# Two stacked sequence blocks on one core: other SBUF byte offsets for weights, rounded activations and hidden tiles, and the meta tokens' rounding moved to the first down product

## The chip, the cores and the metric

The kernel runs as one program on one core of one Trainium2 chip. The metric is the device time of that program in microseconds. Three runs of the kernel before took 1779.9, 1780.93 and 1783.77 us; their median is 1780.93 us.

## What is computed

Two blocks follow each other on 512 tokens of width 1024. The first mixes three branches (gated linear attention, a short convolution, windowed attention), then runs a gated feed-forward net with a causal convolution. The second puts 16 learned meta tokens ahead of the 512, runs two recurrent mixers (HGRN2 and Mamba-2) side by side, then a second feed-forward net. Cut to the matrix products that carry the time:

```python
u = rmsnorm(h, g_mix);  z = u @ w_in                    # 1024 -> 7440
merged = g1 * (o_gla @ w_gla_o) + g2 * (o_conv @ w_conv_o) + g3 * (o_swa @ w_swa_o)
h = h + merged @ w_o
h = h + (silu(conv(u @ w_up)[:, :2816]) * conv(u @ w_up)[:, 2816:]) @ w_down
h = concat([meta_tokens, h])                            # 16 + 512 tokens
proj = rmsnorm(h, norm1) @ w_in_2                       # 1024 -> 6672
h = h + concat([hgrn2(proj), mamba2(proj)]) @ w_out_2
h = h + conv_glu(rmsnorm(h, norm2) @ ffn_w_up) @ ffn_w_down
out = rmsnorm(h, final)[16:]
```

## The kernel before

Activations lie feature-major: 128 features on the partitions, tokens along the row, eight such tiles (index `k`) for the width of 1024. `H` is the residual in float32. Each product is taken in three passes on numbers cut to the engine's float32r format: an operand is split into a rounded high part and the rest (`XH` and `XL` for the normed input, `FH` and `FL` for the hidden layer of a feed-forward net, `MH` and `ML` for the merged branches, `bh_*` with `bl_*` or `blg*` for the three branch outputs, `yh` and `yl` for the mixers' outputs; `wh` and `wl` for the weights).

The weights come as a stream of 128x128 tiles, eight to a chunk of 512 KB. SyncE loads a chunk into `wraw` (line 69), ScalarE rounds it to `wh` (line 82), VectorE takes the rest to `wl` (line 83). A chunk is prepared two chunks before it is used.

`gemm` makes one output tile of 128 features. For each input tile `k` (a "k-step" below) `pass3` issues `(wh, xh)`, `(wh, xl)`, `(wl, xh)`: the weight tile is the stationary operand, and a row of 512 activations moves through it (line 179). So in block 1 a k-step is three matmuls of 512 columns. In block 2 the tokens are cut in two pieces, 256 and 258 columns or 264 and 264, so that a k-step there is six matmuls. Each matmul has a weight load of its own. In the profile a matmul `acc<-XH,wh` has `XH` as its moving operand and `wh` as its stationary one. Only the first product (`GV`) has it the other way round.

The order of the main stages on TensorE is: projections, branches and gates (to about 503 us), `w_up` (503 to 749), `w_down` (749 to 872), projections and mixers of block 2 with pieces of 264 and of 256 + 258 (872 to 1285), `w_out_2` (to 1379), `ffn_w_up_2` (to 1636), `ffn_w_down_2`.

Tiles get their place in SBUF from pools in the order in which the pools are opened and the tiles first asked for: `H`, `XH`, `XL`, the parameters, the constants `cm`, then `wraw`, `wh` and `wl`, then the small `stat` tiles, then whatever the stage needs. A constant or a pad more shifts all that follows it. `XH` and `XL` have a row of 528 tokens for each `k` (2112 bytes): 16 meta tokens in columns 0 to 15, the others from column 16 (`META`).

`split` is one ScalarE activation (high part) and one VectorE operation (rest). `meta_norm` is a generator: it is stepped in lane 1, between the k-steps of the first products, and it first splits the 16 meta columns of the eight `k` and then works out their norm. The calls are recorded, and a scheduler then sets each engine's order. In the first down product, `after(m, ...)` makes the new normed input of block 2 from each finished tile `m`.

Of the kernel before, what the change touches and what calls it, by code (L numbers as in the profile page):

```python
# [9 lines left out]
F32 = mybir.dt.float32  # L10
# [12 lines left out]
L = T + META  # L23
PADL = T + 32
KD = D // P
NFF = 22
# [100 lines left out]
class Builder:  # L127
    def __init__(self, ctx, tc, ins, out):
        self.tc, self.nc, self.ins, self.out = tc, tc.nc, ins, out
        nc = self.nc  # L130
        self.const = ctx.enter_context(tc.tile_pool(reuse_waits="tile", name="const", bufs=1))
        self.wraw = ctx.enter_context(tc.tile_pool(reuse_waits="tile", name="wraw", bufs=2))
        self.whl = ctx.enter_context(tc.tile_pool(reuse_waits="tile", name="whl", bufs=3))
        self.stat = ctx.enter_context(tc.tile_pool(reuse_waits="tile", name="stat", bufs=1))
        self.acc_p = ctx.enter_context(tc.tile_pool(reuse_waits="tile", name="accp", bufs=4, space=PSUM))
        self.sm_p = ctx.enter_context(tc.tile_pool(reuse_waits="tile", name="smp", bufs=4, space=PSUM))
        self.W = WStream(nc, ins["wts"], self.wraw, self.whl)
        self.lanes = [Lane() for _ in range(4)]
        self.hold = False
        self.pend = []  # L140
# [163 lines left out]
    def setup(self):  # L304
# [4 lines left out]
        self.par_t = c.tile([P, NPAR], F32, name="par_t")  # L309
        cm = c.tile([P, 3 * P + 16], F32, name="cm")  # L310
        self.four = cm[:, 3 * P:]
        self.ident, self.le, self.ones = (cm[:, i * P:(i + 1) * P] for i in range(3))
# [8 lines left out]
        nc.gpsimd.dma_start(out=self.par_t[:, 8:NPAR], in_=self.ins["par"][:, 8:NPAR])  # L321
        nc.gpsimd.dma_start(out=cm, in_=self.ins["cm"])
        nc.gpsimd.dma_start(out=self.H[:, :, 0:META], in_=self.ins["metaT"])
# [176 lines left out]
    def block1(self):  # L500
# [16 lines left out]
        for k in range(KD):  # L517
            self.split(XH[:, k, META:L], XL[:, k, META:L], H[:, k, META:L], self.par("g_mix", k))
            if k > 2:
                square(k - 3)  # L520
# [4 lines left out]
        Rx = R[:, META:L]  # L525
        segs = [(META, T)]
        X = self.X()
        WI = lambda c: [("w_in", k, c) for k in range(KD)]

        with ExitStack() as s1:  # L530
            br = self.br = s1.enter_context(tc.tile_pool(reuse_waits="tile", name="br", bufs=1))
            self.BH = {n: br.tile([P, 4, T], F32R, name=f"bh_{n}") for n in ("gla", "conv", "swa")}
            self.BL = {n: br.tile([P, 4, T], F32R, name=f"bl_{n}") for n in ("conv", "swa")}
            blg = self.blg = [None] * 4
# [5 lines left out]
            with ExitStack() as s2:  # L540
# [14 lines left out]
                with tc.tile_pool(reuse_waits="tile", name="sp", bufs=1) as sp:  # L555
# [6 lines left out]
                    for k in range(KD):  # L562
                        wh, wl = self.W.take([("w_in", k, GV + m * P) for m in range(4)])
                        for b in range(4):
                            c = slice(META + b * P, META + (b + 1) * P)
                            for i, (x, w) in enumerate(((XH, wh), (XL, wh), (XH, wl))):
                                self.mm(accs[b], x[:, k, c], w, start=k == 0 and i == 0, stop=k == 7 and i == 2)
# [4 lines left out]
                    def ev_gv(a):  # L572
                        for b in range(4):
# [3 lines left out]
                    self.lanes[1].add(self.meta_norm(), 6)  # L577
                    self.gemm16(wga, self.par("g_mix", 0, KD), segs, 3,
                                lambda a: self.mul(self.GAt[0:96], a[0][0:96], Rx[0:96]))
# [56 lines left out]
            mp = s1.enter_context(tc.tile_pool(reuse_waits="tile", name="mp", bufs=1))  # L636
            MH = mp.tile([P, KD, T], F32R, name="MH")
            ML = mp.tile([P, KD, T], F32R, name="ML")
            for m in range(KD):
# [20 lines left out]
            for m in range(KD):  # L660
                def ev_o(a, m=m):
                    h = H[:, m, META:L]
                    self.add(h, h, a[0])
                    self.split(XH[:, m, META:L], XL[:, m, META:L], h, self.par("g_ffn", m))
                    self.sumsq(sqa, m, h)
# [7 lines left out]
        def after(m, h, _):  # L673
            self.split(XH[:, m, META:L], XL[:, m, META:L], h, g1[:, m:m + 1])
            self.sumsq(sqh, m, h)
            self.ts(h, h, self.par("g_final", m), ALU.mult)
            self.sumsq(sqg, m, h)
# [3 lines left out]
    def ffn(self, up, cw, cb, down, R, after, zero):  # L681
        nc, tc, H = self.nc, self.tc, self.H
        W = T + 2
        segs = [(META, T)] if zero else [(META - 2, 256), (META + 254, 258)]
        Xb = (self.XH, self.XL)
        with tc.tile_pool(reuse_waits="tile", name="fp", bufs=1) as fp:
            FH = fp.tile([P, NFF, T], F32R, name="FH")
            FL = fp.tile([P, NFF, T], F32R, name="FL")
            for j in range(NFF):
                cs = []  # L690
                for i in range(2):
# [6 lines left out]
                    def ev(a, i=i, f=f, u=u, c=c, cs=cs, j=j):  # L698
                        o = 2 if zero else 0
                        for ps, (c0, n) in zip(a, segs):  # L700
                            self.mul(u[:, o:o + n], ps[:, 0:n], R[:, c0:c0 + n])
# [38 lines left out]
    def meta_norm(self):  # L740
        nc, H, st = self.nc, self.H, self.stat
        for k in range(KD):
            self.split(self.XH[:, k, 0:META], self.XL[:, k, 0:META], H[:, k, 0:META], self.par("norm1", k))
            yield 1
        sq = st.tile([P, L], F32, tag="sqt", name="msq", bufs=1)[:, 0:KD * META].rearrange("p (k t) -> p k t", t=META)
# [757 lines left out]
```

## Time and profile before

| | |
|---|---|
| median of three runs | 1780.93 us |
| the profiled execution's own time | 1779.66 us |
| its span | 1777.8 us |
| TensorE (PE) busy | 1747.9 us, 98% |
| weight loads (PEld) busy | 1535.7 us, 86% |
| VectorE (DVE) busy | 1092.6 us, 61% |
| ScalarE (ACT) busy | 728.9 us, 41% |
| moved from HBM | 156.93 MB, 89 GB/s |

The busy time of TensorE counts the union of its matmuls, whose ends are modelled and overlap. What a matmul costs in a dense stream is read from the distance between the starts of two matmuls in the timeline; below that is called the pitch, and the distance between the starts of two k-steps the length of a k-step. The rows round starts to 10 ns, the trace keeps them to 1 ns.

### The profile page before, as it was taken

How to read it: one execution, taken by the hardware profiler on the slowest of the kernel's cores; microseconds unless marked ns; L12 is line 12 of the kernel's file. 1: busy time of each engine (PE TensorE's matmuls, PEld its weight loads, DVE VectorE, ACT ScalarE, POOL GpSimd, SP SyncE). 2: the span in 40 equal slices, each digit the busy share in tenths (PEclk: the TensorE clock that was granted, in tenths of full speed). 3: DMA queues.
4: the chain of work that ended last, by engine and by line, in shares of the span. 5: the costliest groups of instructions: out<-in, count | busy, mean ns of one | idle time of the engine just before them, and what ended most of it. 6: DMA issues, size and time to landing. Idle time of an engine off the chain costs nothing. (4 is left out here: it accounts for less than half of the span.)

```text
span 1777.8 us, 26968 instructions
## 1 busy us (share of the span) xinstructions
PE 1747.9 (98%) x11014; PEld 1535.7 (86%) x11014; DVE 1092.6 (61%) x1923; ACT 728.9 (41%) x1175; POOL 124.8 (7%) x203
## 2 busy tenths in 40 slices
PE   8999999999999999999998999999999999999997
PEld 6777778888888888888898999999999999999775
DVE  5476774444457777733488789767633676676332
ACT  5356342222344444423356545555432444344221
POOL 2000000000110000001112221000001000000000
PEclk9999999999999999999999999999999999999998
DMA  5221223332333333233233322222222223323321
GB/s 184 84 72 60 72 74 93 95 95 93 95 95 95 95 95 95 95 95 95 86 100 128 115 83 72 69 71 69 73 91 88 91 87 93 96 88 91 95 88 66
DMA packets 45691, 160.84 MB, mean 90 GB/s; under 512 B 5472, under 2 KB 5616, under 8 KB 45568
## 3 DMA queue, kind: packets, MB, share of 16 engines
q1 hardware_dynamic: 42480, 149.83, 27.6%
q0 software_dynamic: 2800, 9.03, 1.6%
q8 instruction: 86, 1.41, 0.3%
q14 instruction: 37, 0.30, 0.1%
q10 hardware_dynamic: 288, 0.27, 0.0%
HBM read 156.93 MB, written 2.18 MB: 89 GB/s over the span
## 5 line engine op out<-in xcount | busy, mean ns | idle before, releaser
L179 PE MATMUL acc<-XH,wh 128*128 128x512 f32 (+3 forms) x2320 | 632.2, 326 | 0.1
L179 PE MATMUL acc<-XL,wh 128*128 128x512 f32 (+3 forms) x2320 | 621.6, 321 | 0.0
L179 PE MATMUL acc<-XH,wl 128*128 128x512 f32 (+3 forms) x2320 | 621.5, 322 | 0.0
L82 ACT CAST wh<-wraw 128x1024 fp32r<-128x1024 f32 (+1 forms) x279 | 291.6, 1045 | 520.0 <-PE acc L179 453.5
L83 DVE TENSOR_TENSOR wl<-wraw,wh 128x1024 fp32r<-128x1024 f32 (+1 forms) x279 | 341.7, 1225 | 220.4 <-ACT wh L82 213.3
L179 PEld LDWEIGHTS acc<-XH,wh 128*128 128x128 f32 x2320 | 385.7, 189 | 44.9 <-issue 9.7
L179 PEld LDWEIGHTS acc<-XH,wl 128*128 128x128 f32 x2320 | 386.2, 189 | 33.8 <-issue 0.5
L179 PEld LDWEIGHTS acc<-XL,wh 128*128 128x128 f32 x2320 | 385.5, 188 | 33.0 <-issue 0.5
L179 PE MATMUL acc<-FH,wh 128*128 128x512 f32 x352 | 140.3, 399 | 0.0
L179 PE MATMUL acc<-FH,wl 128*128 128x512 f32 x352 | 138.9, 395 | 0.0
L179 PE MATMUL acc<-FL,wh 128*128 128x512 f32 x352 | 138.6, 394 | 0.0
L162 DVE SCALAR_TENSOR_TENSOR c<-u,par_t,c 128x512 f32<-128x512 f32 x176 | 131.9, 749 | 6.8 <-ACT c L176 3.7
L150 DVE TENSOR_TENSOR u<-acc,R 128x512 f32<-128x512 f32 (+2 forms) x132 | 63.8, 510 | 91.2 <-PE acc L179 88.1
L334 POOL TENSOR_TENSOR sqa<-sqa,sqt 128x512 f32<-128x512 f32 x27 | 40.9, 1515 | 745.9 <-ACT sqt L176 745.9
L179 PEld LDWEIGHTS acc<-FH,wl 128*128 128x128 f32 x352 | 66.1, 188 | 16.5
L179 PEld LDWEIGHTS acc<-FL,wh 128*128 128x128 f32 x352 | 66.1, 188 | 15.6
L179 PEld LDWEIGHTS acc<-FH,wh 128*128 128x128 f32 x352 | 66.1, 188 | 15.3
L176 ACT ACTIVATE FH<-c 128x512 fp32r<-128x512 f32 x44 | 27.8, 632 | 116.5 <-DVE c L150 116.5
L150 DVE TENSOR_TENSOR H<-H,acc 128x512 f32<-128x512 f32 (+2 forms) x41 | 22.6, 569 | 77.7 <-PE acc L179 77.7
L176 ACT ACTIVATE c<-u,par_t 128x512 f32<-128x512 f32 x88 | 67.7, 769 | 2.6 <-DVE u L150 2.5
L176 ACT ACTIVATE c<-c 128x512 f32<-128x512 f32 x44 | 27.8, 632 | 85.1 <-DVE c L162 85.0
L179 PE MATMUL acc<-yh,wh 128*128 128x256 f32 (+1 forms) x256 | 51.4, 283 | 0.1
(393 smaller groups left out, 1969.6 us busy)
## 6 DMA issues: line engine op xcount, KB each, us to landing
wraw<-in_wts SPq DMA_DIRECT2D x277, 512.0 KB, 3.6
seg<-cumd POOLq DMA_DIRECT2D x10, 512.0 KB, 4.5
H<-in_xT SPq DMA_DIRECT2D x8, 256.0 KB, 9.1
ei<-eid POOLq DMA_DIRECT2D x16, 128.0 KB, 3.2
out<-H SPq DMA_DIRECT2D x7, 256.0 KB, 2.7
wraw<-in_wts SPq DMA_DIRECT2D x2, 256.0 KB, 4.4
r<-in_r POOLq DMA_DIRECT2D x1, 272.0 KB, 3.7
r<-in_r POOLq DMA_DIRECT2D x1, 256.0 KB, 7.5
```

What stands on the lines that cost most here:

```text
L82: self.nc.scalar.copy(h[:, e], t[:, e])
L83: self.nc.vector.tensor_tensor(out=l[:, e], in0=t[:, e], in1=h[:, e].bitcast(F32), op=ALU.subtract)
L150: self.nc.vector.tensor_tensor(out=out, in0=a, in1=b, op=op)
L162: self.nc.vector.scalar_tensor_tensor(out=out, in0=a, scalar=s, in1=b, op0=op0, op1=op1)
L176: self.nc.scalar.activation(out=out, in_=a, func=func, scale=scale, **kw)
L179: self.nc.tensor.matmul(out, lhsT, rhs, start=start, stop=stop)
L334: self.nc.gpsimd.tensor_tensor(out=acc, in0=acc, in1=t, op=ALU.add)
```

## The change

Five pieces of layout change, and one piece of work moves.

- `cm` has 8 columns more (32 bytes), which are never used. All that lies behind it moves up by 32 bytes: `wraw`, `wh`, `wl`.
- `stat` gets a pad of 160 bytes; what lies behind it moves by 192 bytes in all.
- A pad of 512 bytes stands between the high and the low tiles of the branches, of `M` and of `F`.
- In block 1 the rounded input lies in columns 8 to 519 of `XH` and `XL` (`X1 = 8`) and no longer in 16 to 527. Block 2 uses the columns it used before.
- Since columns 8 to 15 then hold tokens of block 1, the split of the 16 meta tokens can't stand in `meta_norm` any longer. It is made tile by tile in `after` of the first down product.

```diff
+X1 = 8
...
+        self.stat.tile([P, 40], F32, name="pad0")
...
-        cm = c.tile([P, 3 * P + 16], F32, name="cm")
-        self.four = cm[:, 3 * P:]
+        cm = c.tile([P, 3 * P + 24], F32, name="cm")
+        self.four = cm[:, 3 * P:3 * P + 16]
...
-        nc.gpsimd.dma_start(out=cm, in_=self.ins["cm"])
+        nc.gpsimd.dma_start(out=cm[:, 0:3 * P + 16], in_=self.ins["cm"])
...
-            self.split(XH[:, k, META:L], XL[:, k, META:L], H[:, k, META:L], self.par("g_mix", k))
+            self.split(XH[:, k, X1:X1 + T], XL[:, k, X1:X1 + T], H[:, k, META:L], self.par("g_mix", k))
...
-        segs = [(META, T)]
+        segs = [(X1, T)]
...
             self.BH = {n: br.tile([P, 4, T], F32R, name=f"bh_{n}") for n in ("gla", "conv", "swa")}
+            br.tile([P, P], F32, name="pad1")
...
             MH = mp.tile([P, KD, T], F32R, name="MH")
+            mp.tile([P, P], F32, name="pad2")
             ML = mp.tile([P, KD, T], F32R, name="ML")
...
         def after(m, h, _):
             self.split(XH[:, m, META:L], XL[:, m, META:L], h, g1[:, m:m + 1])
+            self.split(XH[:, m, 0:META], XL[:, m, 0:META], H[:, m, 0:META], self.par("norm1", m))
...
-        segs = [(META, T)] if zero else [(META - 2, 256), (META + 254, 258)]
+        segs = [(X1, T)] if zero else [(META - 2, 256), (META + 254, 258)]
+        rsegs = [(META, T)] if zero else segs
...
             FH = fp.tile([P, NFF, T], F32R, name="FH")
+            fp.tile([P, P], F32, name="pad3")
             FL = fp.tile([P, NFF, T], F32R, name="FL")
...
     def meta_norm(self):
         nc, H, st = self.nc, self.H, self.stat
-        for k in range(KD):
-            self.split(self.XH[:, k, 0:META], self.XL[:, k, 0:META], H[:, k, 0:META], self.par("norm1", k))
-            yield 1
```

The two built programs give each tile its byte address in a partition. From these, for each product, the offset of the moving row from the weight tile, taken modulo 256 bytes (all `wh` and `wl` buffers lie a multiple of 4096 bytes apart, and weight tiles 512 bytes, so there is one offset for each row):

| moving rows | start modulo 256, before | offset from the weights, before | start, after | offset, after |
|---|---|---|---|---|
| `wh`, `wl` themselves | 192 | | 224 | |
| `XH`, `XL` in block 1, `k` = 0, 1, 2, 3 (then again) | 192, 0, 64, 128 | 0, 64, 128, 192 | 160, 224, 32, 96 | 192, 0, 64, 128 |
| `bh`, `bl`, `blg`, `MH`, `ML`, `FH`, `FL` | 32 | 96 | 224 | 0 |
| `XH`, `XL` in block 2, pieces of 264 | 128 + 64k; 160 + 64k | 192 + 64k; 224 + 64k | the same | 160 + 64k; 192 + 64k |
| `XH`, `XL` in block 2, pieces of 256 and 258 | 184 + 64k | 248, 56, 120, 184 | the same | 216, 24, 88, 152 |
| `yh8` to `yh15` | 32 and up by 32 | 96, 128, 160, 192, 224, 0, 32, 64 | 224 and up by 32 | 0, 32, ... 224 |
| `yh0` to `yh7` | 160 and up by 64 | 224, 32, 96, 160 (twice) | 96 and up by 64 | 128, 192, 0, 64 (twice) |

From `XH` to `XL` it is 16,896 bytes before and after (512 modulo 1024); between the high and low tiles of `M` and `F` it was a multiple of 1024, and is now 512 bytes more.

The order of TensorE's matmuls is the same, but for the two matmuls of the meta tokens' norm, which stand some 25 rows earlier. On the two engines that make the splits, the order changes at the start and at the end of `w_up`.

VectorE at the start of the program, from the third chunk of weights on, before (`XL<-H,par_t,XH 128x16` is a meta split, `sqa<-sqa,R` adds a square to the sum for the norm, `wl<-wraw,wh` is the low part of a chunk):

```order
L83 TENSOR_TENSOR wl<-wraw,wh 128x1024
L162 SCALAR_TENSOR_TENSOR XL<-H,par_t,XH 128x512 x4
L516 TENSOR_TENSOR sqa<-sqa,R 128x512
L162 SCALAR_TENSOR_TENSOR XL<-H,par_t,XH 128x512
L516 TENSOR_TENSOR sqa<-sqa,R 128x512
L83 TENSOR_TENSOR wl<-wraw,wh 128x1024
L516 TENSOR_TENSOR sqa<-sqa,R 128x512
L162 SCALAR_TENSOR_TENSOR XL<-H,par_t,XH 128x16
L83 TENSOR_TENSOR wl<-wraw,wh 128x1024
L162 SCALAR_TENSOR_TENSOR XL<-H,par_t,XH 128x16 x6
```

and the same place after:

```order
L84 TENSOR_TENSOR wl<-wraw,wh 128x1024
L164 SCALAR_TENSOR_TENSOR XL<-H,par_t,XH 128x512 x4
L518 TENSOR_TENSOR sqa<-sqa,R 128x512
L164 SCALAR_TENSOR_TENSOR XL<-H,par_t,XH 128x512
L518 TENSOR_TENSOR sqa<-sqa,R 128x512 x2
L84 TENSOR_TENSOR wl<-wraw,wh 128x1024 x2
```

The seven meta splits here are gone, and the third sum now stands ahead of the chunk's low part instead of behind it.

ScalarE at the same place, before (`R<-H` and `sqt<-H` are squares, `wh<-wraw` rounds a chunk):

```order
L176 ACTIVATE XH<-H,par_t 128x512 x2
L176 ACTIVATE R<-H 128x512
L176 ACTIVATE XH<-H,par_t 128x512 x3
L176 ACTIVATE R<-H 128x512
L176 ACTIVATE XH<-H,par_t 128x16 x2
L82 CAST wh<-wraw 128x1024
L176 ACTIVATE sqt<-H 128x512
L176 ACTIVATE R<-H 128x512
```

and after:

```order
L178 ACTIVATE XH<-H,par_t 128x512
L178 ACTIVATE R<-H 128x512
L178 ACTIVATE XH<-H,par_t 128x512 x3
L178 ACTIVATE R<-H 128x512
L178 ACTIVATE XH<-H,par_t 128x512
L178 ACTIVATE R<-H 128x512
L83 CAST wh<-wraw 128x1024
L178 ACTIVATE sqt<-H 128x512
```

The rounding of the chunk now stands behind the third square instead of two meta splits.

VectorE at the end of `w_up`, after (`c` is a convolution's sum; before, the `128x16` rows are not there and the rest stands in the same order):

```order
L164 SCALAR_TENSOR_TENSOR c_5417<-u,par_t,c_5417 128x512
L164 SCALAR_TENSOR_TENSOR XL<-H,par_t,XH 128x16
L164 SCALAR_TENSOR_TENSOR c_5417<-u,par_t,c_5417 128x512
L164 SCALAR_TENSOR_TENSOR XL<-H,par_t,XH 128x16 x6
L152 TENSOR_TENSOR u<-acc,R 128x512
L84 TENSOR_TENSOR wl<-wraw,wh 128x1024
L164 SCALAR_TENSOR_TENSOR c_5456<-u,par_t,c_5456 128x512
L164 SCALAR_TENSOR_TENSOR XL<-H,par_t,XH 128x16
```

The scheduler has pulled the eight meta splits from `after` ahead, to the last two column groups of `w_up`.

## Rows read from the trace of the kernel before

**Rows 1.** The page, busy time, share of the span and instructions of each engine.

```profile
PE 1747.9 (98%) x11014; PEld 1535.7 (86%) x11014; DVE 1092.6 (61%) x1923; ACT 728.9 (41%) x1175; POOL 124.8 (7%) x203
```

**Rows 2.** Window of `w_down`: busy us of PE, PEld, DVE, ACT, POOL, granted clock, DMA.

```profile
749.10:872.20 123.10, 123.10 (x529) 99.05 (x528) 49.14 (x48) 36.97 (x45) 17.07 (x12) 1.00 0.31 94
```

**Rows 3.** Groups by line and shape: count, busy us, mean ns, idle before.

```profile
L179 PE MATMUL acc<-XH,wh 128*128 128x512 f32 x784 | 312.5, 399 | 0.0
L179 PE MATMUL acc<-FH,wh 128*128 128x512 f32 x352 | 140.3, 399 | 0.0
L179 PE MATMUL acc<-MH,wh 128*128 128x512 f32 x64 | 25.5, 399 | 0.0
L179 PE MATMUL acc<-bh_gla,wh 128*128 128x512 f32 x32 | 12.7, 398 | 0.0
L179 PE MATMUL acc<-XH,wh 128*128 128x256 f32 x544 | 156.4, 288 | 0.0
```

**Rows 4.** Timeline of TensorE, gates of block 1: start us, length, engine, line.

```profile
443.80 0.39 PE L179 MATMUL acc<-XH,wh 128*128 128x512 f32 x1
...
444.49 0.40 PE L179 MATMUL acc<-XH,wh 128*128 128x512 f32 x1
...
445.19 0.40 PE L179 MATMUL acc<-XH,wh 128*128 128x512 f32 x1
...
445.89 0.39 PE L179 MATMUL acc<-XH,wh 128*128 128x512 f32 x1
...
446.58 0.39 PE L179 MATMUL acc<-XH,wh 128*128 128x512 f32 x1
```

**Rows 5.** Timeline of TensorE, `w_down`: starts of its first two column groups.

```profile
749.09 0.39 PE L179 MATMUL acc<-FH,wh 128*128 128x512 f32 x1
...
764.48 0.40 PE L179 MATMUL acc<-FH,wh 128*128 128x512 f32 x1
```

**Rows 6.** Timeline of TensorE, `w_out_2`: starts of `yh8` to `yh15`, `yh0`, next group.

```profile
1356.26 0.40 PE L179 MATMUL acc<-yh,wh 128*128 128x256 f32 x2
...
1356.97 0.40 PE L179 MATMUL acc<-yh,wh 128*128 128x256 f32 x2
...
1357.70 0.40 PE L179 MATMUL acc<-yh,wh 128*128 128x256 f32 x2
...
1358.40 0.40 PE L179 MATMUL acc<-yh,wh 128*128 128x256 f32 x2
...
1359.13 0.40 PE L179 MATMUL acc<-yh,wh 128*128 128x256 f32 x2
...
1361.98 0.40 PE L179 MATMUL acc<-yh,wh 128*128 128x256 f32 x2
...
1367.70 0.40 PE L179 MATMUL acc<-yh,wh 128*128 128x256 f32 x2
```

**Rows 7.** Timeline of TensorE, `ffn_w_up_2`: two starts that lie 32 k-steps apart.

```profile
1503.17 0.40 PE L179 MATMUL acc<-XH,wh 128*128 128x256 f32 x2
...
1526.32 0.40 PE L179 MATMUL acc<-XH,wh 128*128 128x256 f32 x2
```

**Rows 8.** Timeline at the start, TensorE: a matmul that waited for weights.

```profile
20.45 0.50 PE L179 MATMUL acc<-wl,XH 128*128 128x512 f32 x1 [0.64 <-DVE wl L83]
```

**Rows 9.** Timeline at the start, VectorE: a sum of squares, the weights' low part.

```profile
17.31 0.69 DVE L516 TENSOR_TENSOR sqa<-sqa,R 128x512 f32<-128x512 f32 x1
...
19.18 1.22 DVE L83 TENSOR_TENSOR wl<-wraw,wh 128x1024 fp32r<-128x1024 f32 x1
```

**Rows 10.** Timeline at the start, ScalarE: two meta splits, the weights' high part.

```profile
17.60 0.49 ACT L176 ACTIVATE XH<-H,par_t 128x16 fp32r<-128x16 f32 x2
18.00 1.03 ACT L82 CAST wh<-wraw 128x1024 fp32r<-128x1024 f32 x1
```

**Rows 11.** Timeline of VectorE: six meta splits early; the last hidden tile.

```profile
23.24 1.99 DVE L162 SCALAR_TENSOR_TENSOR XL<-H,par_t,XH 128x16 fp32r<-128x16 f32 x6
...
754.28 0.69 DVE L150 TENSOR_TENSOR FL<-c,FH 128x512 fp32r<-128x512 f32 x1 [0.70 <-ACT FH L176]
```

More of the change, by code (lines that the diff above doesn't have):

```diff
@@ L564, in block1 @@
                         for b in range(4):
-                            c = slice(META + b * P, META + (b + 1) * P)
+                            c = slice(X1 + b * P, X1 + (b + 1) * P)
                             for i, (x, w) in enumerate(((XH, wh), (XL, wh), (XH, wl))):
@@ L577, in block1 @@
                     self.lanes[1].add(self.meta_norm(), 6)
-                    self.gemm16(wga, self.par("g_mix", 0, KD), segs, 3,
+                    self.gemm16(wga, self.par("g_mix", 0, KD), [(META, T)], 3,
                                 lambda a: self.mul(self.GAt[0:96], a[0][0:96], Rx[0:96]))
@@ L663, in ev_o @@
                     self.add(h, h, a[0])
-                    self.split(XH[:, m, META:L], XL[:, m, META:L], h, self.par("g_ffn", m))
+                    self.split(XH[:, m, X1:X1 + T], XL[:, m, X1:X1 + T], h, self.par("g_ffn", m))
                     self.sumsq(sqa, m, h)
@@ L699, in ev @@
                         o = 2 if zero else 0
-                        for ps, (c0, n) in zip(a, segs):
+                        for ps, (c0, n) in zip(a, rsegs):
                             self.mul(u[:, o:o + n], ps[:, 0:n], R[:, c0:c0 + n])
```

## The prediction

> **What bounds the kernel now.** I read the busy shares first. TensorE has a matmul in flight for 98% of the span, VectorE and ScalarE for 61% and 41% [rows 1]; a stage view of `w_down` shows the same picture with the full granted clock of 1.00, which is the upper of TensorE's two levels, 2.4 GHz [rows 2]. So the time is the sum of TensorE's pitches, and other engines count only where TensorE waits for them. Next I read the timeline for the pitch itself. At 2.4 GHz 512 columns would take 213.3 ns. A column group of `w_down` has 22 k-steps of three matmuls and takes 764.48 - 749.09 = 15.39 us, 233 ns a matmul [rows 5]. No engine is named as releaser in there, and the length repeats: of 336 undisturbed k-steps of `w_down`, 332 take 700 ns to the nanosecond. So some 20 ns of each matmul is surplus that no wait explains.
>
> Then I asked what changes the surplus. In block 1 the k-steps on `XH` and `XL` have the same three matmuls of 512 columns, but a cycle of lengths: 690, 698, 697 and 695 ns for `k` = 0, 1, 2, 3, the same for 4 to 7, and so on through all of `w_up` (0.69, 0.70, 0.70, 0.69 in the rounded rows [rows 4]; the first value stands in 163 of 179 undisturbed steps). What goes round with period four in `k` is the address of the moving row: a row of 2112 bytes moves it by 64 modulo 256. The weights meanwhile move by 512 a step, and `FH` by 2048 while its pitch never changes. So a period of 256 bytes fits, and I take the offset of the moving row from the weight tile loaded beside it as the variable. The tables of the change then say what is wanted: offset 0 gives 690 ns, 64, 128 and 192 give 698, 697 and 695, and 96 gives 700, the worst seen in these steps.
>
> **The change part by part.**
>
> *Branches, `M` and `F`: offset from 96 to 0.* There are 352 k-steps on `F`, 64 on `M` and 3 x 32 on the branches [rows 3], 512 in all. The nearest row for offset 0 is the first step of the `XH` cycle, 690 ns [rows 4], against 700 now [rows 5]. 512 x 10 ns = **-5.1 us**. Bounds: if the 690 belongs to its place in the cycle and not to its offset, these steps get the cycle's mean, 695, which is -2.6; if the fourth step's luck is better, 687 ns (three pitches of 229, the best steady stretch I find, in the first product at 17 to 19 us), -6.7. The pads of 512 bytes cost nothing themselves. They leave offsets modulo 256 as they are, so in this sum they are worth nothing either.
>
> *`XH` and `XL` in block 1.* The rows go down by 32 bytes and the weights up by 32: the offsets are 192, 0, 64, 128, the same four values in the same order, one step later. The cycle of 2.78 us for four steps [rows 4] should stay: **0**, with 784 k-steps [rows 3] at stake, 1.6 us either way for 2 ns a step. The pieces of 264 in block 2 swap the offsets of their two halves: 0.
>
> *`XH` and `XL` in pieces of 256 and 258.* These are 544 k-steps [rows 3], most of them in `ffn_w_up_2`, where 32 take 23.15 us, 723 ns each [rows 7]. Their offsets now lie 8 bytes below multiples of 64, and will lie 8 bytes below odd multiples of 32. The trace has no step like that, and the neighbours are the steps of `w_out_2`, which have the same shapes on `yh` and `yl`. There the high tile's offset climbs by 32: 96, 128, 160, 192 take 0.71, 0.73, 0.70 and 0.73 us [rows 6]. Over all sixteen tiles the odd multiples of 32 average 714 ns and the multiples of 64 721. The steps in question, at 723, are like the latter; moved to the former they would gain 7.6 ns. 544 x 7.6 = **-4.1 us**. The ends are 0 (the 8 bytes matter more than the rest, since no `yh` starts there) and 20 ns a step, the distance to the best `yh` step, -10.9. I take the middle value, as the mean of twelve rows.
>
> *`w_out_2`.* `yh8` to `yh15` keep their set of offsets. `yh0` to `yh7` now stand on odd multiples of 32 and take (1367.70 - 1361.98) / 8 = 715 ns [rows 6]; they come to multiples of 64, 721. 64 steps x 6 ns = **+0.4 us**.
>
> *The start.* TensorE waits 0.64 us for a chunk's low part [rows 8]. That operation runs 19.18 to 20.40 on VectorE [rows 9], behind the chunk's rounding on ScalarE, 18.00 to 19.03 [rows 10]. Now the third square stands ahead of the rounding in place of two meta splits. It reuses the buffer that the sum of 17.31 reads until 18.00 [rows 9], so it runs 18.0 to 18.6, the rounding 18.6 to 19.6, and the low part, behind the third sum, 19.8 to 21.0. **+0.6 us**; 0 if the square finds its buffer earlier. Later chunks have some microseconds to spare, and the norm's matmuls are only moved to where their inputs are long done.
>
> *The moved meta splits.* Eight on ScalarE, eight on VectorE. Six took 1.99 us on VectorE [rows 11], so eight are 2.7 us there, less on ScalarE, and no DMA or other queue. They now stand in the last two column groups of `w_up`. Behind them on ScalarE waits the rounding of a chunk that is needed two chunks later; behind them on VectorE waits the last hidden tile, finished at 754.97 [rows 11] and needed in the last k-step of the group that ends at 764.48 [rows 5]. With 2.7 us more it still has 6: 0. Without that cover it would be 2.7.
>
> The sum: -5.1 - 4.1 + 0.4 + 0.6 = **-8.2 us**. Against the profiled execution's own 1779.66 that is 1771.5. The median of the runs is 1.3 higher, so on that footing I expect **1772.7 us**.
>
> **The rivals.** A measurement of this kernel tells about 0.2%, or 3.6 us, from no change.
>
> *Only the hidden tiles gain.* The 8 bytes decide the pieces of 256 and 258, and nothing is won there: -4.1, 1776.8. For it: their four steps do not rank as the `yh` steps do (the one at offset 184 is the slowest, 735 ns).
>
> *Addresses don't matter.* The differences are those of the tensors, or of the place in the stream, and only the start shows: +0.6, 1781.5. Against it speaks the cycle of four in `XH` [rows 4], which has one tensor, one shape and nothing else that goes round by four. The Trainium skill, "TensorE: Matmul & The Clock Gate", section "Step-by-step: what each phase is for", says so by its rule: moving operand and weight load have a read port each, and loading the next weights takes nothing from the running matmul. By that rule the time would be that of this rival; the trace does not agree, as far as the cycle is a matter of addresses.
>
> *Slower: the start within 64 bytes.* Suppose the mechanism is not the distance but where a row starts: rows at 0 modulo 64 (`XH` in block 1, 695 on average) against rows at 32 modulo 64 (`F`, `M`, branches, 700). The change puts all of block 1's `XH` rows at 32 modulo 64 and leaves the others there: 784 x 5 ns = +3.9, with the start +4.5, 1785.4. It decides if the fetch of a row pays for the piece it shares with its neighbour. Against it: the `yh` steps that start at 32 modulo 64 are the faster ones [rows 6], and the halves of 264, one at 0 and one at 32, have the same mean pitch within 0.5 ns.
>
> **How the numbers follow.** The forecast gets 0.46, the hidden tiles alone 0.21, no effect 0.17, slower 0.09; 0.07 are left for a larger gain than any row shows, by the pads or by the steady stretches settling better, around 1764. Faster by over 0.2% is below 1777.4: 0.95 of the forecast, 0.6 of the second case, and the large gain, 0.63 in all. Slower by over 0.2% is the one rival, 0.09. The rest, 0.28, is within. The range goes from 1764.5, with the good ends of both main terms (-6.7 and -10.9) less what else is uncertain, to 1782.5, which takes in the case without effect. The forecast's own range is 1766 to 1777.
>
> **What would show it.** The k-steps of `w_down` should take 690 ns, a column group 15.2 us instead of 15.39, and those of the gates and `w_up` still cycle with 2.78 us for four. 32 k-steps of `ffn_w_up_2` should take 22.9 us instead of 23.15. At the start TensorE should wait about 1.2 us for `wl` near 20 us. If `w_down` stays at 700 the offset is the wrong variable. If four steps on `XH` take 2.80 or more, the start within 64 bytes was the cause. A wait of TensorE near 764 us would show that the meta splits were not covered.

## The result and the profile after

The changed kernel takes **1769.26 us** (median of four runs, 1768.26 to 1771.67) against 1780.95 before (1779.90 to 1783.77); the ratio is 0.9936, with a 95% interval from 0.9924 to 0.9949. That is 11.4 us less, where 8.2 were forecast; the time lies in the forecast's own range.

The profiled execution took 1771.67 us, the slowest of its four, with a span of 1769.8 us against 1777.8. So the two traces differ by 8.0 us only, and the reason stands in the table: TensorE runs the same 9360 products of rounded operands in the same order in both kernels, so the start of each can be set against its counterpart. The differences, by stage:

| stage | before, us | after, us | difference | forecast |
|---|---|---|---|---|
| to the end of the first product | 36.80 | 38.56 | +1.8 | +0.6 |
| projections, branches, `M` (64 + 96 k-steps at 700) | 465.76 | 463.12 | -2.6 | -1.6 |
| `w_up` (352 k-steps on `XH`) | 246.53 | 246.53 | 0.0 | 0 |
| `w_down` (176 k-steps on `FH`) | 123.20 | 119.73 | -3.5 | -1.8 |
| block 2 up to `w_out_2` | 412.39 | 413.79 | +1.4 | -1.5 |
| `w_out_2` | 94.48 | 94.35 | -0.1 | +0.4 |
| `ffn_w_up_2` (352 k-steps of 256/258) | 257.11 | 254.83 | -2.3 | -2.7 |
| `ffn_w_down_2` to the end (176 k-steps on `FH`) | 141.55 | 138.94 | -2.6 | -1.8 |

(The forecast's two main terms are shared out here by k-steps.) The line that does not fit is the stage of block 2 with its many small operations, +1.4. There TensorE waits for VectorE at the same three places in both traces. First before, then after; the columns are start, length, engine, line, operation, and in brackets the wait with its releaser:

```profile
955.53 0.77 PE L182 MATMUL sm<-cm,xf 128*128 128x128 f32 x5 [1.92 <-DVE xf L162]
966.26 0.77 PE L182 MATMUL sm<-cm,xf 128*128 128x128 f32 x5 [1.51 <-DVE xf L162]
977.34 0.77 PE L182 MATMUL sm<-cm,xf 128*128 128x128 f32 x5 [1.88 <-DVE xf L162]
```

```profile
951.87 0.77 PE L184 MATMUL sm<-cm,xf 128*128 128x128 f32 x5 [2.75 <-DVE xf L164]
962.66 0.77 PE L184 MATMUL sm<-cm,xf 128*128 128x128 f32 x5 [1.58 <-DVE xf L164]
973.92 1.09 PE L184 MATMUL sm<-cm,xf 128*128 128x128 f32 x5 [2.08 <-DVE xf L164]
```

The waits are 1.1 us longer. The rest comes from the granted clock. 0.3 us after the end of the third wait it fell to 0.50, the lower of TensorE's two levels (1.2 GHz), for 3.4 us, while before kept 1.00 here; so the five matmuls of the last row take 1.09 us instead of 0.77. The same stretch of matmuls, from the end of this wait on, takes 2.66 us before (first row) and 4.24 after (second row); the third row is the time at the lower level:

```profile
977.34:980.00 2.66, 2.66 (x28) 2.33 (x29) 2.62 (x4) 2.63 (x8) 0.00 (x0) 1.00 0.29 34
973.92:978.16 4.24, 4.24 (x29) 3.71 (x29) 2.75 (x4) 2.99 (x8) 0.00 (x0) 0.60 0.42 124
974.23:977.64 3.41, 3.41 (x26) 3.05 (x24) 2.22 (x3) 2.68 (x7) 0.00 (x0) 0.50 0.45 125
```

In all, the stretch from 872 to 1000 us of before's time is 2.4 us longer. The profiles of the kernels below sort by this fall of the clock and not by their addresses: the two without one (`e2_pad0`, `e5_x16`) have the stretch 0.7 to 0.8 us shorter than before, the three with one or two falls in it have it longer, by 1.2 (`e7_row576_8`), 1.3 (`e4_weights`) and, with two falls and nothing but before's addresses, 3.1 us (`e3_move`). In `e6_row576` the fall comes behind the stretch, which is 0.6 us shorter. The mean granted clock of the changed kernel's other three executions, 1768.26 to 1769.91 us, is 0.998, where this one has 0.997. So I do not count this stretch to the change. Without it the stages give -10.4 for this pair of executions, and the medians -11.7.

Now the profile itself. Busy shares, to be set beside [rows 1]: 9.9 us less of TensorE, the rest as before.

```profile
PE 1738.0 (98%) x11014; PEld 1534.6 (87%) x11014; DVE 1089.8 (62%) x1923; ACT 729.7 (41%) x1175; POOL 123.9 (7%) x203
```

Groups by line and shape (busy us, mean ns of one), answering [rows 3]: `XH` with 512 columns is as it was, `FH` falls from 399 to 392 ns (its mean holds steps that had not settled, too), `MH` from 399 to 389.

```profile
L181 PE MATMUL acc<-XH,wh 128*128 128x512 f32 x784 | 312.5, 399 | 0.0
L181 PE MATMUL acc<-FH,wh 128*128 128x512 f32 x352 | 137.8, 392 | 0.0
L181 PE MATMUL acc<-MH,wh 128*128 128x512 f32 x64 | 24.9, 389 | 0.0
```

Timeline of TensorE. In `w_down` the first column group lasts from 748.21 to 763.22, 15.01 us instead of 15.39 [rows 5]; the two k-steps behind it take 680 ns each (763.22 to 763.90, 763.90 to 764.58), where 690 was forecast. The gates still cycle: four k-steps last from 443.70 to 446.48, 2.78 us as in [rows 4].

```profile
748.21 0.39 PE L181 MATMUL acc<-FH,wh 128*128 128x512 f32 x1
...
763.22 0.39 PE L181 MATMUL acc<-FH,wh 128*128 128x512 f32 x1
...
763.90 0.39 PE L181 MATMUL acc<-FH,wh 128*128 128x512 f32 x1
...
764.58 0.39 PE L181 MATMUL acc<-FH,wh 128*128 128x512 f32 x1
```

```profile
443.70 0.40 PE L181 MATMUL acc<-XH,wh 128*128 128x512 f32 x1
...
446.48 0.40 PE L181 MATMUL acc<-XH,wh 128*128 128x512 f32 x1
```

And in `ffn_w_up_2` the 32 k-steps of [rows 7] take 1521.98 - 1499.05 = 22.93 us instead of 23.15, 717 ns each.

```profile
1499.05 0.28 PE L181 MATMUL acc<-XH,wh 128*128 128x256 f32 x1
...
1521.98 0.28 PE L181 MATMUL acc<-XH,wh 128*128 128x256 f32 x1
```

### The profile page after: what moved, and what is told of

Read it like the earlier page. It is cut to its first block, busy times and chain, and to the rows that moved or that the text cites. A ratio compares the mean times of both kernels' runs of the same rounds, so it can differ in the third digit from the quotient of the medians.

```text
span 1769.8 us, 26970 instructions
## 1 busy us (share of the span) xinstructions
PE 1738.0 (98%) x11014; PEld 1534.6 (87%) x11014; DVE 1089.8 (62%) x1923; ACT 729.7 (41%) x1175; POOL 123.9 (7%) x203
## 2 busy tenths in 40 slices
DMA packets 45691, 160.84 MB, mean 91 GB/s; under 512 B 5472, under 2 KB 5616, under 8 KB 45568
## 5 line engine op out<-in xcount | busy, mean ns | idle before, releaser
L181 PEld LDWEIGHTS acc<-FL,wh 128*128 128x128 f32 x352 | 66.1, 188 | 13.5
```

Of the source, the lines that this page charges most:

```text
L181: self.nc.tensor.matmul(out, lhsT, rhs, start=start, stop=stop)
```

## Experiments

The forecast's variable, the offset between moving row and weights modulo 256 bytes (the *distance* from here on), fits the stages. But the steps at distance 0 take 680 ns, and the `XH` step at the same distance 690. The changed kernel differs in one more way there: its pads put 512 bytes between high and low tiles. So the theory to test is that the distance alone sets the pitch; the rivals are the pads, the address of the row by itself, and something that has nothing to do with addresses.

### The price of a distance by itself

A kernel with the model left out runs streams of k-steps, three matmuls each, over one buffer. In its core the start of the rows (`a`), of the weights (`b`), the row length and the low rows' offset (`ld`) are free, in units of four bytes:

```
for k in range(ks):
    wo = W0 + b + (k % 8) * P
    wh, wlo = S[:, wo:wo + P], S[:, wo + wl:wo + wl + P]
    xo = X0 + a + (k % 8) * row
    for i, (w, x) in enumerate(((wh, xo), (wh, xo + ld), (wlo, xo))):
        ...
            nc.tensor.matmul(acc[:, 0:m], w, S[:, x + c0:x + c0 + m], ...
```

> A kernel of fp32r matmuls alone, with none of the model in it (the output is a copy of one accumulator, not the reference's): streams of k-steps of three matmuls as in the kernel, with the moving rows at a bytes and the weights at b bytes modulo 256, both in steps of 32, then finer steps of a, other distances between high and low rows, rows of 2112 bytes, and pieces of 256/258 and 264. Theory 'distance': the pitch goes by a - b modulo 256 alone; streams that keep a - b = 0 take 680 ns a k-step, those that keep 96 take 700, and rows of 2112 bytes give the cycle 690, 698, 697, 695. Rival 'own address': the step goes by a alone, the eight values of b agree within 1 ns. Rival 'pads': at a - b = 0 a distance of 45056 bytes between high and low rows gives 690 and 45568 gives 680. Rival 'not addresses': all streams of 512 columns take the same within 2 ns.

Measured, from the starts of the matmuls in its trace. Each stream is 24 matmuls; the value is the mean of its last four k-steps, in ns, and the range goes over eight pairs of `a` and `b` with the same distance, spread over all of 0 to 224 (seven for 0; the first stream, behind an idle TensorE, is left out). Sixteen more streams, at odd multiples of 8 bytes, lie between 693 ns (at 40, 88 and 248) and 713 (at 168):

| distance | 0 | 32 | 64 | 96 | 128 | 160 | 192 | 224 |
|---|---|---|---|---|---|---|---|---|
| lowest | 680 | 700 | 686 | 700 | 695 | 701 | 700 | 700 |
| highest | 682 | 700 | 687 | 701 | 700 | 704 | 700 | 700 |

The windows that hold one stream each, distance 0 first, then 96; the columns are the length, then busy us and (instructions) of TensorE, its weight loads, VectorE, ScalarE and GpSimd, the granted clock, and the DMA share. Both have the 24 matmuls of a stream and the tail of the one before; the full clock is granted; the first is 0.15 us shorter.

```profile
219.72:225.17 5.45, 5.45 (x25) 4.50 (x24) 0.69 (x1) 0.00 (x0) 0.00 (x0) 1.00 0.00 0
236.29:241.89 5.60, 5.60 (x25) 4.51 (x24) 0.69 (x1) 0.00 (x0) 0.00 (x0) 1.00 0.00 0
```

So the distance counts, and where the two stand by themselves does not, to within 5 ns (at 128 one of the eight pairs takes 695 and seven take 700): the rival of the own address falls, and with it the slower case of the prediction (rows at 32 modulo 64). The pads fall as well: at distance 0 a gap of 45056 bytes between high and low rows gives 680, and 45568 gives 680. What remains is the row length. With rows of 2112 bytes from distance 0 on the stream settles on 690, 699, 696, 695, and from 64 on on 698, 697, 695, 690, the kernel's cycle to within 1 ns. So the 690 is the price of distance 0 *on the way through the cycle*; a stream that stays at 0 takes 680. Nor is a step's length set by its own distance modulo 256 alone: with rows of 2176 bytes, which alternate between 0 and 128, the stream settles on four lengths, 704, 694, 697 and 692.

### The offset of `F`, `M` and the branches alone

```diff
+        self.stat.tile([P, 40], F32, name="pad0")
```

> The kernel before with 160 bytes more in the pool of statistics, so that F, M and the branches stand at distance 0 from the weights; rows, weights, order and the distance between high and low tiles (45056 bytes for F) as before. Theory 'distance': k-steps of F, M and two branches take 680 ns instead of 700, 480 x 20 ns = -9.6 us, with the steps on yh within 1 us of before: 1770 to 1772 us. Rival 'pads': the 512 bytes between high and low tiles, not here, gave the second half; steps of 690, -5.1 us, 1776. Rival 'own address': rows start at 192 modulo 256 here and at 224 in the changed kernel; some third value of the step, or 700 and no change.

Measured: 1773.19 us, ratio 0.9958 (0.9945 to 0.9970). In the trace 316 of 340 undisturbed k-steps on `FH` take 680 ns, all 64 on `MH` and all on two of the branches too; there are no pads between high and low tiles. `w_down` takes 119.70 us. So the theory holds in the kernel too, and the pads buy nothing (of the third branch, `bh_gla`, half of the steps take 680 and half 690).

Of the 9.6 us expected 7.5 show by the ratio, and 9.0 between the two profiled executions' spans, neither of which has a fall of the clock near 1000 us. One place in the trace tells where some of it went: `ffn_w_up_2` became 1.1 us *slower* (258.23 against 257.11), though not one address of its matmuls differs from before. Its steps settle on 728, 720, 730, 728 for the four distances (`k` = 1, 2, 3, 0) where before they settled on 721, 718, 735, 719. Here are 32 of its k-steps, 23.25 us against the 23.15 of [rows 7]:

```profile
1496.28 0.29 PE L180 MATMUL acc<-XH,wh 128*128 128x256 f32 x1
...
1519.53 0.29 PE L180 MATMUL acc<-XH,wh 128*128 128x256 f32 x1
```

### Moving the meta splits alone

```diff
     def after(m, h, _):
         self.split(XH[:, m, META:L], XL[:, m, META:L], h, g1[:, m:m + 1])
+        self.split(XH[:, m, 0:META], XL[:, m, 0:META], H[:, m, 0:META], self.par("norm1", m))
 ...
     def meta_norm(self):
-        for k in range(KD):
-            self.split(self.XH[:, k, 0:META], self.XL[:, k, 0:META], H[:, k, 0:META], self.par("norm1", k))
-            yield 1
```

> The kernel before with only the eight meta splits moved to the first down product; no address changes. Theory: the start loses about 1.4 us, as in the trace of the changed kernel (two waits of TensorE near 20 us instead of one), the eight splits at the end of w_up cost 0: +1.4 us, 1782.3. Rival (as predicted): +0.6 at the start. Rival: the splits in w_up are not covered, +2.7 more.

Measured: 1780.70 us, ratio 1.0000 (0.9991 to 1.0009). But this run does not test what it was made for. ScalarE's timeline at the start still has the meta splits there (the second line):

```profile
17.29 0.62 ACT L176 ACTIVATE R<-H 128x512 f32<-128x512 f32 x1
17.81 0.49 ACT L176 ACTIVATE XH<-H,par_t 128x16 fp32r<-128x16 f32 x2
18.20 1.04 ACT L82 CAST wh<-wraw 128x1024 fp32r<-128x1024 f32 x1
```

With the rows at column 16 nothing binds the meta columns, and the scheduler takes the splits back to the start wherever they are written. In the changed kernel it is the overlap of the rows (from column 8) with the meta columns that keeps them late. The price of the move is read two experiments further on.

### The weights 32 bytes up, alone

```diff
-        cm = c.tile([P, 3 * P + 16], F32, name="cm")
+        cm = c.tile([P, 3 * P + 24], F32, name="cm")
...
```

> The kernel before with the constants' tile 32 bytes longer: weights and all behind them go up by 32, the rows XH and XL stay. F, M, branches and yh keep their distance (96) from the weights: steps of 700. XH in block 1 comes to odd multiples of 32 (224, 32, 96, 160), where no row of before stands; the pieces of 256/258 come to 8 below odd multiples of 32, as in the changed kernel. Theory 'distance': pieces 544 x (723 to 717) = -3 us, and 784 steps of XH between 687 and 700 instead of 695, -6 to +4 us; in all -9 to +1 us. Rival 'own address': XH rows did not move, its steps stay 690, 698, 697, 695 and the pieces 723: 0.

Measured: 1779.76 us, ratio 0.9996 (0.9987 to 1.0005). The terms nearly cancel: `ffn_w_up_2` goes from 257.11 to 254.85 us, all of what the changed kernel has (254.83), while `w_up` goes from 246.53 to 247.10, the rest of block 1 grows by 0.9, and block 2 up to `w_out_2`, where the clock fell once in this execution, by 0.8. On odd multiples of 32 the undisturbed steps on `XH` take 697.2 ns on average, against 695.2 before. In `w_up` they settle on a cycle of eight, 713, 687, 698, 691, 699, 701, 694, 691, though the distances go round by four. `F`, `M` and two of the branches stay at 700. So the pieces' gain comes from the weights' shift by itself, and the start column 8 is what keeps `XH` from paying for it.

### The changed kernel with the rows at column 16

```diff
-X1 = 8
+X1 = 16
```

> The changed kernel with the rounded rows at column 16 of their buffer again instead of 8; pads, weights, F, M and branches as in the changed kernel. The rows no longer overlap the meta columns, so the scheduler puts the meta splits back to the start. Theory: TensorE waits about 1.2 us less near 20 us, the steps on XH in block 1 come to odd multiples of 32 and take 697 instead of 695.7 on average (784 x 1.6 = +1.3 us), F, M and two branches stay at 680, the pieces of 256/258 stay: 1769.3 within 1 us. Rival 'the meta splits were what was gained' : 3 us or more slower than the changed kernel. Rival 'start only': 1.2 us faster, XH stays at 695.7.

Measured: 1770.41 us, ratio 0.9946 (0.9933 to 0.9960); the changed kernel's interval, 0.9924 to 0.9949, overlaps with this one. `w_up` takes 247.10 us again, `w_down` 119.69, `ffn_w_up_2` 254.83. At the start the meta splits are back and TensorE runs through: the first product ends 1.5 us sooner than in the changed kernel, 2.0 counted from the first matmul. About 1.0 of that is input that landed later in the changed kernel's profile (see "The start" below), so that column 8 costs 0.5 to 1.1 us at the start; it gives back 1.2 in block 1 (0.57 in `w_up`, 0.58 before it). Which of the two is faster these times do not tell.

The rows of `XH` and the weights stand here as in `e4_weights`, and the cycle of eight comes again, but with its other half first. The step on `k` = 0 of the same column group, first there (713 ns), then here (699):

```profile
639.12 0.40 PE L179 MATMUL acc<-XH,wh 128*128 128x512 f32 x1
...
639.83 0.39 PE L179 MATMUL acc<-XH,wh 128*128 128x512 f32 x1
```

```profile
636.44 0.40 PE L181 MATMUL acc<-XH,wh 128*128 128x512 f32 x1
...
637.14 0.39 PE L181 MATMUL acc<-XH,wh 128*128 128x512 f32 x1
```

So with 512 columns, too, one address can have two lengths.

### Pieces of 256 and 258, 264, and low rows elsewhere

> A second kernel of fp32r matmuls alone, with none of the model in it (the output is a copy of one accumulator). All rows keep one distance from the weights through a stream. First 512 columns with the high rows at a and the low rows at dl more, both modulo 256 in steps of 32; then pieces of 256/258 with a in steps of 4 bytes, 264/264 in steps of 8, the splits 256/272 and 272/256, and 256/256. Theory 'the distance of each operand counts, and equal distances of 0 are the best': no cell of the first grid is below 680 ns, the row dl = 0 repeats 680, 699, 687, 700, 700, 703, 700, 700, others lie between 685 and 715; pieces of 256/258 repeat 700 at 144 and 176 and lie at 700 to 743 elsewhere. Rival 'the values of pieces are accidents of what ran before': 144 and 176 do not repeat 700 within 2 ns after another predecessor.

Measured, mean of the last four k-steps of a stream. First grid (512 columns): no cell is below 680, and 680 stands only where high and low rows are both at 0; the row `dl` = 0 reads 680, 700, 687, 700, 700, 703, 700, 700. The pieces of 256/258 lie between 700 and 740, with neighbours four bytes apart up to 35 ns apart; 176 has 700 again, and 184 has 740. The windows of these two streams, 48 matmuls each:

```profile
638.29:643.89 5.60, 5.60 (x50) 5.60 (x49) 0.85 (x2) 0.00 (x0) 0.00 (x0) 1.00 0.00 0
649.72:655.55 5.83, 5.83 (x50) 5.83 (x49) 0.85 (x2) 0.00 (x0) 0.00 (x0) 1.00 0.00 0
```

But 144 does not repeat: 700 in the first probe and 707 here; 8 gives 720 there and 700 here, 64 gives 720 and 710, 128 gives 727 and 710. The other 19 of the 23 distances that both probes have agree within 2 ns. So the theory holds for 176, and 144 is as the rival has it: some distances have more than one settled length. What selects one stays open between the probes, which differ in what ran before and in the gap between high and low rows too (16896 and 18432 bytes, both 0 modulo 256). In `e2_pad0` the gap and all addresses of the pieces are those of before, and still they settled elsewhere; there what ran before differs, and so do the addresses of other engines' tiles, which lie 160 bytes up. No run parts the two.

### A row length that keeps the distance

If the cycle of `XH` comes from rows of 2112 bytes, rows of 2304 (nine times 256) end it. The rest of the edit makes room: the pads go, and a table of 1 KB moves into a buffer that is free at that time.

```diff
-X1 = 8
+X1 = 34
+ROW = 576
...
-        self.XH = c.tile([P, KD, L], F32R, name="XH")
-        self.XL = c.tile([P, KD, L], F32R, name="XL")
+        self.XH = c.tile([P, KD, ROW], F32R, name="XH")[:, :, 6:ROW]
+        self.XL = c.tile([P, KD, ROW], F32R, name="XL")[:, :, 6:ROW]
...
-        cm = c.tile([P, 3 * P + 24], F32, name="cm")
+        cm = c.tile([P, 3 * P + 40], F32, name="cm")
```

> The changed kernel with rows of XH and XL of 2304 bytes instead of 2112, so that the distance from the weights no longer moves with k: 0 for the 512 columns of block 1 (which start at column 34, behind the meta columns), 176 for the pieces of 256/258, 120 for those of 264. F, M and branches stay at 0; the pads between high and low tiles are gone, the table of the attention's distances is loaded later into another buffer, and the meta splits are back at the start. Theory 'distance': steps on XH in block 1 take 680 ns instead of 696 on average (784 x about 15 = -11.5 us), pieces of 256/258 700 instead of 717 where they run undisturbed (544 x 14 to 17 = -8 to -9 us), pieces of 264 740 instead of 731 (+1.5), the start about 1 us less: 1749 to 1752 us. Rival 'the cycle is a matter of the tensor or of the change of weights': steps on XH keep a cycle of four, the time stays at 1768 to 1770.

The second kernel of this pair differs in two numbers, the start column and the start of the rows in their buffer:

```diff
-X1 = 34
+X1 = 32
...
-        self.XH = c.tile([P, KD, ROW], F32R, name="XH")[:, :, 6:ROW]
-        self.XL = c.tile([P, KD, ROW], F32R, name="XL")[:, :, 6:ROW]
+        self.XH = c.tile([P, KD, ROW], F32R, name="XH")[:, :, 8:ROW]
+        self.XL = c.tile([P, KD, ROW], F32R, name="XL")[:, :, 8:ROW]
```

> The kernel of the run beside it (rows of 2304 bytes) with one thing moved: rows start 8 bytes further on in their buffer and the 512 columns of block 1 two columns earlier, so that these keep distance 0 and every matmul of 512 columns stands as there, while the pieces of 256/258 come from distance 176 to 184 and those of 264 from 120 to 128. The instructions and their order are the same. Theory 'distance': pieces of 256/258 take 740 ns instead of 700 where undisturbed, 544 x 30 to 40 = +16 to +22 us against the run beside it, 264 unchanged (740). Rival 'distance counts for 512 columns only, or only in steps of 32 bytes': the same time within 1 us.

Measured: **1755.10 us**, ratio 0.9856 (0.9842 to 0.9869), for the first, the fastest kernel of this study, 14 us below the changed one; and 1769.71, ratio 0.9939 (0.9925 to 0.9952), for the second, which runs the same instructions in the same order with some rows 8 bytes elsewhere. The steps on `XH` with 512 columns: 662 of 713 undisturbed ones take 680 ns, and four of them 439.37 to 442.09, 2.72 us where the cycle took 2.78 [rows 4].

```profile
439.37 0.39 PE L181 MATMUL acc<-XH,wh 128*128 128x512 f32 x1
...
442.09 0.39 PE L181 MATMUL acc<-XH,wh 128*128 128x512 f32 x1
```

The stages of the first kernel in windows, `w_up`, `w_down`, `ffn_w_up_2`, and then the same of the changed kernel. The counts of TensorE are the same:

```profile
496.49:737.91 241.42, 241.42 (x1073) 199.91 (x1072) 174.84 (x229) 106.28 (x134) 6.05 (x43) 1.00 0.32 96
737.91:857.59 119.68, 119.68 (x529) 99.10 (x528) 49.01 (x48) 37.11 (x46) 16.91 (x13) 1.00 0.32 97
...
1364.61:1613.63 249.02, 249.02 (x2134) 248.82 (x2133) 178.21 (x283) 109.02 (x135) 1.85 (x1) 1.00 0.31 94
```

```profile
501.68:748.21 246.53, 246.53 (x1073) 200.05 (x1072) 175.90 (x236) 107.94 (x141) 6.02 (x43) 1.00 0.30 94
748.21:867.94 119.73, 119.73 (x529) 99.10 (x528) 49.15 (x50) 37.24 (x47) 16.94 (x12) 1.00 0.31 97
...
1376.08:1630.91 254.83, 254.83 (x2134) 254.64 (x2133) 178.72 (x283) 107.48 (x135) 1.85 (x1) 1.00 0.29 92
```

`ffn_w_up_2` gives 5.8 us more (352 x 16.5 ns) and `w_up` 5.1 (352 x 14.5). With the pieces at 184 that stage takes 262.86 us, 13.8 us more than at 176 (352 x 39 ns). Thirty-two k-steps of it, first at 176, then at 184, 22.40 and 23.68 us:

```profile
1484.84 0.28 PE L181 MATMUL acc<-XH,wh 128*128 128x256 f32 x1
...
1507.24 0.28 PE L181 MATMUL acc<-XH,wh 128*128 128x256 f32 x1
```

```profile
1493.99 0.29 PE L181 MATMUL acc<-XH,wh 128*128 128x256 f32 x1
...
1517.67 0.29 PE L181 MATMUL acc<-XH,wh 128*128 128x256 f32 x1
```

The first kernel stays 3 us above the 1749 to 1752 expected: the start did not recover (TensorE waits 1.13 us there), the undisturbed steps on pieces of 264 average 746 ns instead of 740 (51 take 740, and 44 take 760 at the same distance), and from the first product to `w_up` 4.9 us came where 432 steps x 15 are 6.5. The second is 14.6 us above the first (16.5 us by the spans), a little under the 16 to 22 expected: in the rest of block 2, where VectorE ends many waits, only 2.8 us of the loss show.

## Why the prediction was right, and where it was off

**The bound and the variable.** TensorE's pitch was the bound, and the distance modulo 256 between moving row and weights moves it: shown by the first probe (same distance, same length within 5 ns, wherever both stand), by `e2_pad0`, and by `e6_row576` against `e7_row576_8`. It does not fix it alone: the distances of steps before count (690 in the cycle, 680 in a stream), and `e4_weights` and `e5_x16` have two lengths at one address. Why the distance matters no run shows. The Trainium skill, "TensorE: Matmul & The Clock Gate", section "Step-by-step: what each phase is for", gives the moving operand and the weight load a read port each; by that rule alone, no distance would differ from another. The probes do not agree: 680 to 704 ns for 512 columns, with next to nothing else running but the copies that empty the accumulators.

**`F`, `M` and the branches: mis-sized by half.** The term was -5.1 us, from 700 to 690; it measured 20 ns a step: 352 on `FH` (-7.0), 64 on `MH` (-1.3) and 96 on the branches, of which the 32 of `bh_gla` got 7 ns only (-1.5; 18 ns in `e5_x16`, at the same addresses); together -9.8, of which some 0.9 us near the end of `ffn_w_down_2` went into waits. The step that failed is the reading of the first step of the `XH` cycle as *the* price of distance 0: it is the price of passing through it. Even the good end of the bounds, 687, came from a stretch that stays at 64 (687 in the probe). And the trace of before did hold the value: in the first product the last k-step at distance 0 that no wait disturbs goes from 21.95 to 22.63, 680 ns.

```profile
21.95 0.39 PE L179 MATMUL acc<-wl,XH 128*128 128x512 f32 x1
22.18 0.39 PE L179 MATMUL acc<-wh,XH 128*128 128x512 f32 x1
22.40 0.39 PE L179 MATMUL acc<-wh,XL 128*128 128x512 f32 x1
22.63 0.39 PE L179 MATMUL acc<-wl,XH 128*128 128x512 f32 x1
```

Four steps stand at this distance there; the first is cut by the wait, the next two take 695 and 690, and the last has settled. The prediction took its values from long stretches and passed over this short one. (The 336 steps that it counts in `w_down` are those of both down products; `w_down` has 176.)

**`XH` in block 1: right.** `w_up` takes 246.53 us in both kernels, and the cycle is the same four values.

**Pieces of 256 and 258: right in the long stream, by luck, and too large elsewhere.** 723 to 715.5 was forecast, 717 came in `ffn_w_up_2`, which gave 2.3 us of the 2.7 expected. The first probe has both cycles: with rows of 2112 bytes its pieces settle on 721, 718, 735, 719 from 56 on and on 715, 715, 722, 715 from 24 on, as the kernel does before and after. The other 192 steps stand in short runs between other work and gave 1.4 ns each (153 undisturbed ones), 0.3 us where 1.5 was forecast; the step that failed there is the price of a long stream put on short runs. The pieces of 264, put at 0, gained 2.1 ns a step (178 undisturbed ones), 0.5 us for 224. The reasoning behind the term, "odd multiples of 32 are better", is not a rule: the second probe shows neighbours four and eight bytes apart that differ by up to 40 ns.

**`w_out_2`: nothing.** +0.4 was forecast, -0.1 came; the steps on `yh` move by up to 14 ns either way.

**The start: the right mechanism and about its size, and 1.0 us of late input beside it.** +0.6 was forecast, +1.6 came (1.8 less 0.2 by which the first matmul was later). The chain is the one of the forecast: ScalarE's third square waits for the sum that frees its buffer, the rounding stands behind the square, the low part behind the rounding and the third sum, and TensorE waits for both parts. The time of that sum is what came out otherwise: 18.00 was taken from the trace of before as its end, 18.99 came. VectorE's order up to the sum is the same as before. The work ahead of it begins with a tile of `H` that landed later in this execution; ScalarE rounds it at 13.47 before (first row) and at 14.42 after (second row), and the sum starts 3.84 us behind it before (17.31 [rows 9]) and 3.88 after:

```profile
13.47 1.34 ACT L176 ACTIVATE XH<-H,par_t 128x512 fp32r<-128x512 f32 x2 [0.86 <-DMA H<-in_xT]
```

```profile
14.42 0.72 ACT L178 ACTIVATE XH<-H,par_t 128x512 fp32r<-128x512 f32 x1 [0.94 <-DMA H<-in_xT]
...
18.30 0.69 DVE L518 TENSOR_TENSOR sqa<-sqa,R 128x512 f32<-128x512 f32 x1
...
19.09 0.63 ACT L178 ACTIVATE R<-H 128x512 f32<-128x512 f32 x1 [0.45 <-DVE sqa L518]
...
19.63 1.03 ACT L83 CAST wh<-wraw 128x1024 fp32r<-128x1024 f32 x1
...
20.71 0.51 PE L181 MATMUL acc<-wh,XH 128*128 128x512 f32 x1 [0.54 <-ACT wh L83]
...
20.97 1.22 DVE L84 TENSOR_TENSOR wl<-wraw,wh 128x1024 fp32r<-128x1024 f32 x1
...
22.24 0.50 PE L181 MATMUL acc<-wl,XH 128*128 128x512 f32 x1 [0.80 <-DVE wl L84]
```

TensorE waits twice, 0.54 us for the high part and 0.80 for the low part, where it waited once for 0.64 [rows 8] and about 1.2 was forecast. With the input 0.95 us sooner the term would have been some 0.7 (an estimate: 1.6 - 0.95). The seven other profiles of the kernel, before among them, have ScalarE at this tile between 13.02 and 13.68. Nothing in the change touches that transfer, but there is one profile of the changed kernel, so that the delay belongs to this execution alone is not shown.

**The moved meta splits: covered, as forecast.** `w_up` lost nothing, and no wait of TensorE stands near 764 us of before's time.

By the terms then: -9.8 (`F`, `M`, branches) - 2.6 (pieces of 256 and 258) - 0.5 (pieces of 264) - 0.1 + 1.6 = -11.4, or -10.5 with the 0.9 of waits, and again some -11.4 without the late input, beside -11.4 measured by the ratio, whose interval goes from -9.1 to -13.5. The forecast's -8.2 lies above that interval: `F`, `M` and the branches gave 4.7 us more than forecast, the pieces of 264 and `w_out_2` 0.5 each, the pieces of 256 and 258 gave 1.5 less, and the start cost 1.0 more. The pieces' rival (hidden tiles only) and the case without effect are excluded by `e4_weights` and the first probe, the slower one by the probe's grid.

## What to carry to other kernels

Where a long stream of matmuls has a pitch above columns over clock and no wait in it, plot the length of a step against the distance of its operands modulo a power of two before looking for a busy engine; then choose row lengths that keep the distance constant, and not only start addresses. Read the price of a state from a stretch that stays in it: a value taken from a cycle is that of the passage. And before a stage's difference between two profiles is put down to a change, look at the granted clock in it and at when its input landed: 1.6 us of clock and 1.0 us of input stood against the gain here, and a single profile shows them like everything else.

## What the runs showed of the hardware that was not expected

- At the full granted clock, three matmuls of 512 columns over rows with a constant distance, in steps of 32 bytes, settle on 680 to 704 ns, by that distance and, within 5 ns, not by where row and weights stand; with high and low rows both at 0 from the weights it is 680 (but 692 to 700 when the low weights alone stand 32, 64 or 128 bytes off), and none of the 64 combinations of high and low distance in steps of 32 bytes is below it.
- Pieces of 256 and 258 columns are sensitive to four bytes: 700 ns at 176, 727 at 180, 740 at 184, 707 at 188.
- Settled lengths prefer steps of 20 ns: of the 135 streams of pieces in the second probe whose end is seen, 105 take a whole multiple of 20 ns (to within 1 ns) for their last six k-steps together, and 700, 720 and 740 are among the most frequent single values.
- The same distances can settle on two lengths. In the probes 144 bytes gave 700 and 707, 8 bytes 720 and 700; at the same addresses of rows and weights the step on `k` = 0 took 713 ns in `e4_weights` and 699 in `e5_x16`. What selects one was not tried by itself.
- Behind waits of TensorE the granted clock fell to 0.50 for 3.4 us in some executions: in five of the eight profiles of the kernel, between 941 and 1016 us, once or twice. The same matmuls took 1.6 us more in the changed kernel's profile. Waits much like these (1.92, 1.51 and 1.88 us before, 2.75, 1.58 and 2.08 after) stand in profiles without a fall and with one; what decides was not tried.
